# Where the on-chip tiles of a decoder block start: attention's operands 64 bytes apart modulo 128, the down projection's not

## The chip, the cores and the metric

One core of one Trainium2 chip runs the whole kernel. The metric is device time in microseconds (us) of one launch. The kernel before took 448.41 us in the median of three runs (447.92 to 448.52).

## The reference: what is computed

One decoder block on 256 tokens of 1024 channels, all in float32. Cut to what matters here:

```python
h = rmsnorm(x, attn_norm)
proj = h @ w_in                       # latents, MoBA q/k/v, gates
q = rmsnorm(q_lat) @ w_uq             # MLA: 8 heads, 128 plain + 64 rotary features
kv = rmsnorm(kv_lat) @ w_ukv
y_a = causal_attention(q_a, k_a, v_a) @ w_o_mla
y_b = moba_attention(rope(qb), rope(kb), vb) @ w_o_moba   # 256 tokens: one block, so causal attention
x = x + (g_a * y_a + g_b * y_b) @ w_out
h = rmsnorm(x, ffn_norm)
u = causal_dwconv(h @ w_up, conv_w, conv_b)               # 2 x 2816 features
x = x + (silu(u[..., :2816]) * u[..., 2816:]) @ w_down
return rmsnorm(x, final_norm)
```

## The kernel before, in words

Every float32 operand of a matmul is split into a high part in the format fp32r and the rest as a second fp32r tile (`split`, L343: ScalarE casts, VectorE subtracts). A product is then three matmuls, high by high, high by low, low by high (`mm3`, L338). All PE work is made of these triples, besides the transposes of the softmax (float32, with the identity matrix as moving operand) and a few small products.

A matmul has a stationary operand (`lhsT`, 128 columns, brought into the array by a weight load, which the profile shows as engine PEld) and a moving operand (`rhs`, 128, 256 or 512 columns, streamed through). The weight load of the next matmul runs while the current one streams.

Weights come from HBM in units of 1 MB (`unit_plan`) into a ring of three `raw` tiles, and are split into rings of three `whi` and three `wlo` tiles (L329). The stages, with who is stationary and who moves:

- Projections of the input, queries, keys, gates, output products of attention and the up projection (`proj_pair`, `first_unit`, `mqk_unit`, `up_unit`): the weights `whi`/`wlo` are stationary, activations move, 256 columns at a time. The activations are `XH`/`XL`, `LT`, `YBH`/`YBL`, `VH`/`VL`.
- Values and the projection `out` (`proj_tokens`, `mv_unit`): activations are stationary, weights move, 512 columns.
- Attention (`attention`, L592): eight calls of two heads each. Scores: queries (`qh`/`ql`, `qph`/`qpl`) are stationary, keys (`kh`/`kl`, `krh`/`krl`) move, 128 or 256 columns; the rotary scores of MLA take both heads at once, 256 or 512 columns. Values: `VH`/`VL` or `XH`/`XL` (which hold MLA's values then) are stationary, the transposed probabilities `ph`/`pl` move, 256 and 128 columns.
- The down projection (`down`, L835): 11 units of 24 matmuls. The gated products of two feature tiles lie in the ring tiles `qh`/`ql` (L874), which attention no longer needs; they are stationary, and `whi`/`wlo` move, 512 columns. Each unit stands between two units of the up projection; the last two stand together at the end.

The order on each engine is made by `Program.emit` (L208 on) from costs and dependencies; addresses have no part in it. L243 is the one line that issues all of it, so the profile gives that line to nearly every instruction, and groups are told apart by their tiles' names.

A tile takes its place in the order in which it is made, from byte 16512 of each partition (129 times 128) on, its size rounded up to 32 bytes. `T` (L311) and `Ring` (L314) make tiles where the program first asks for them. All sizes but few are multiples of 128 bytes, so nearly every tile starts at one of two remainders modulo 128. In the kernel before:

| start modulo 128 | tiles |
|---|---|
| 0 | `raw`, `whi`, `wlo`, `cst` (tables, identity, mask) |
| 64 | `XH`, `XL`, `VH`, `VL`, `LT`, `YBH`, `YBL`, `qh`, `ql`, `kh`, `kl`, `qph`, `qpl`, `krh`, `krl`, `ph`, `pl`, `e`, `gate`, `ones`, `prm` and the rest |
| 32 | `warm`, `mhalf`, `first` |

The slices that matmuls read start at multiples of 512 bytes within a tile, so that an operand has the remainder of its tile. Two operands are called of one kind here where the remainders are equal, and of two kinds where they are 0 and 64.

Of the kernel before, what the change touches and what calls it, by code (L numbers as in the profile page):

```python
# [20 lines left out]
F32 = mybir.dt.float32  # L21
F32R = mybir.dt.float32r
BF16 = mybir.dt.bfloat16
# [4 lines left out]
D = 1024  # L28
S = 256
H = 8  # L30
# [4 lines left out]
KT = D // 128  # L35
FT = DFF // 128
UNIT = 2048
# [3 lines left out]
NPAR = P_CB + 2 * FT  # L41
# [262 lines left out]
def hybrid_block(ctx: ExitStack, tc: tile.TileContext, x, par, con, fnorm, wpack, out):  # L304
    ctx.enter_context(tc.manual_schedule())
    sb = ctx.enter_context(tc.tile_pool(name="sb", bufs=1))
    ps = ctx.enter_context(tc.tile_pool(name="ps", bufs=1, space=bass.MemoryType.PSUM))
    P = Program(tc.nc)
    act, dve, pool, pe, sp = P.act, P.dve, P.pool, P.pe, P.sp

    def T(name, shape, dt=F32):  # L311
        return sb.tile([128] + shape, dt, tag=name, name=name)

    class Ring:  # L314


        def __init__(self, name, n, shape, dt=F32, space=None):
            self.n = 0
            self.tiles = [(space or sb).tile([128] + shape, dt, tag=f"{name}{j}", name=f"{name}{j}")
                          for j in range(n)]  # L320

        def __call__(self):
            self.n += 1
# [40 lines left out]
    def groups(wv, k, c):  # L364
        return [t.rearrange("p (m k c) -> p m k c", k=k, c=c) for t in wv]

    cst = T("cst", [4 * S + 258])
    cos1, sin1, cos2, sin2 = (cst[:, S * i : S * i + S] for i in range(4))
    ident = cst[:, 4 * S : 4 * S + 128]
# [1 line left out]
    sel = cst[:, 4 * S + 256 :]  # L371


    warm = sb.tile([128, 512], BF16, tag="warm", name="warm")
    pool.memset(warm, 0.0)
    mhalf = T("mhalf", [4])
    pool.memset(mhalf, -0.5)
    ones = T("ones", [128])
    pool.memset(ones, 1.0)
    o = av_bank()  # L380
# [2 lines left out]

    prm = T("prm", [NPAR])
    act.dma_start(prm[:, :KT], par[:, :KT])
    first = T("first", [4])
    act.activation(first, mhalf, AF.Exp)
    xh, xl = T("XH", [KT, S], F32R), T("XL", [KT, S], F32R)

# [31 lines left out]
    smalls = T("smalls", [192])  # L421
    used = [0]

    def small(n):
        used[0] += n
        return smalls[:, used[0] - n : used[0]]

    diag = Ring("diag", 2, [128])
# [64 lines left out]
    gate = T("gate", [16, S])  # L493
# [38 lines left out]
    rbc, c1, s1 = (T(t, [S]) for t in ("rbc", "c1", "s1"))  # L532
# [29 lines left out]
    for j, n in enumerate((QL, KVL)):  # L562
        c = slice(2 * j, 2 * j + 2)
        t = small(2)
# [8 lines left out]
    for f in range(5):  # L573
        g = prm[:, P_QN + f : P_QN + f + 1]
        j = int(f >= 3)
# [5 lines left out]
    krh, krl = (T(t, [2, S], F32R) for t in ("krh", "krl"))  # L581
# [70 lines left out]
    for i in range(4):  # L652
        qh, ql, kh, kl = qhs(), qls(), khs(), kls()
# [78 lines left out]
    for i in range(4):  # L732
        p = slice(2 * i, 2 * i + 2)
        o = proj_pair("oa", i, yah, yal)
        ta = tas()
# [182 lines left out]
```

## Time and profile before

| | |
|---|---|
| median of three runs | 448.41 us (447.92 to 448.52) |
| the profiled execution | 448.98 us |
| its span, first to last instruction | 447.2 us, mean granted TensorE clock 0.994 |
| PE busy (matmuls) | 436.6 us, 98% of the span, 3299 |
| PEld busy (weight loads) | 412.6 us |
| VectorE, ScalarE busy | 356.7 us, 273.3 us |
| PE's share of the chain that ended last | 92% |

PE's busy time counts overlapping matmuls as one stretch, and a matmul's duration includes the way through the array; what a matmul costs in a stream is the time from its start to the next one's start. That interval is read from the timeline, which gives start times to 0.01 us: over many matmuls from the first and the last row and their count.

### The profile page before, as it was taken

The numbers are of one execution on the slowest core, as the hardware profiler recorded it, in microseconds if no ns is written. First come the engines' busy times: TensorE is split into PE (matmuls) and PEld (weight loads), VectorE is DVE, ScalarE is ACT, GpSimd is POOL, SyncE is SP. The second block draws the span as 40 slices with busy tenths as digits, with TensorE's granted clock in tenths as the row PEclk, the third lists the DMA queues.
The fourth block names the chain that finished last, engine by engine and source line by source line (L and its number), as shares of the span: only waits on it lengthen the run. The fifth ranks groups of instructions, "written<-read, shape, count | busy, mean of one in ns | idle before, by whom it ended". The sixth has DMA issues, their size and how long they took to land.

```text
span 447.2 us, 8109 instructions
## 1 busy us (share of the span) xinstructions
PE 436.6 (98%) x3299; PEld 412.6 (92%) x3299; DVE 356.7 (80%) x544; ACT 273.3 (61%) x469; POOL 11.6 (3%) x26
## 2 busy tenths in 40 slices
PE   7999999999999999999999999999999999999992
PEld 5988999999999999999998899999999999999981
DVE  4768998898879987993788569998797797797764
ACT  5686547456645776787665658765565565565523
POOL 0012200000000000000000010000000000000002
PEclk9999999999999999999999999999999999999997
DMA  7985745445453443250478355386555555556002
GB/s 282 394 332 191 281 161 205 141 155 188 139 182 119 152 160 125 94 190 3 164 308 333 136 189 188 102 301 215 191 205 193 198 198 190 188 189 234 2 0 94
DMA packets 12852, 81.75 MB, mean 183 GB/s; under 512 B 1552, under 2 KB 1936, under 8 KB 4112
## 3 DMA queue, kind: packets, MB, share of 16 engines
q1 hardware_dynamic: 12672, 81.25, 50.1%
q8 instruction: 25, 0.41, 0.4%
q14 instruction: 11, 0.09, 0.1%
q10 hardware_dynamic: 144, 0.00, 0.0%
HBM read 80.20 MB, written 1.05 MB: 182 GB/s over the span
## 4 chain that ended last, share of the span: by engine, by line
PE 92%; DVE 2%; DMA 1%; POOL 1%; ACT 1%; issue 1%; SPq 0%; POOLq 0%; ACTq 0%
PE mm L243 66%; PE av L243 14%; PE sc L243 12%; DMA raw<-in_wpack 1%; DVE wlo L243 1%; POOL smalls L243 1%; ACT tb L243 0%; DVE VL L243 0%; SPq L243 0%; DVE gate L243 0%; DVE tb L243 0%; ACT whi L243 0%; ACT B L243 0%; POOLq L913 0%; DVE diag L243 0%
## 5 line engine op out<-in xcount | busy, mean ns | idle before, releaser
L243 DVE TENSOR_TENSOR wlo<-raw,whi 128x1024 fp32r<-128x1024 f32 (+3 forms) x153 | 175.7, 1162 | 35.2 <-ACT whi L243 34.5
L243 ACT CAST whi<-raw 128x1024 fp32r<-128x1024 f32 (+3 forms) x152 | 151.2, 1008 | 84.1 <-PE mm L243 67.4
L243 PE MATMUL mm<-XH,whi 128*128 128x256 f32 x656 | 183.2, 279 | 0.2 <-ACT XH L243 0.2
L243 PE MATMUL mm<-XH,wlo 128*128 128x256 f32 x656 | 181.7, 277 | 0.7 <-DVE wlo L243 0.7
L243 PE MATMUL mm<-XL,whi 128*128 128x256 f32 x656 | 181.6, 277 | 0.1
L243 PEld LDWEIGHTS mm<-XH,whi 128*128 128x128 f32 x656 | 123.2, 188 | 1.5 <-ACT XH L243 1.1
L243 PEld LDWEIGHTS mm<-XH,wlo 128*128 128x128 f32 x656 | 123.2, 188 | 1.1 <-DVE wlo L243 1.1
L243 PEld LDWEIGHTS mm<-XL,whi 128*128 128x128 f32 x656 | 123.4, 188 | 0.8 <-DVE XL L243 0.3
L243 DVE SCALAR_TENSOR_TENSOR tb<-ta,prm,tb 128x255 f32<-128x255 f32 x88 | 40.5, 481 | 2.2 <-ACT tb L243 0.7
L243 ACT ACTIVATE tb<-ta,prm 128x256 f32<-128x256 f32 x44 | 24.2, 595 | 3.8 <-DVE ta L243 3.8
L243 ACT ACTIVATE e<-sc,smalls 128x128 f32<-128x128 f32 (+1 forms) x32 | 13.3, 419 | 12.8 <-DVE smalls L243 11.9
L243 ACT CAST qh<-ta 128x256 fp32r<-128x256 f32 (+1 forms) x26 | 11.4, 437 | 12.3 <-DVE ta L243 12.2
L243 DVE TENSOR_TENSOR ta<-ta,tb 128x256 f32<-128x256 f32 (+1 forms) x35 | 16.9, 484 | 2.2 <-ACT ta L243 0.7
L243 DVE TENSOR_TENSOR ta<-mm,rbc 128x512 f32<-128x512 f32 x22 | 15.2, 690 | 4.2 <-PE mm L243 4.2
L243 PE MATMUL mm<-YBH,whi 128*128 128x256 f32 x64 | 18.1, 283 | 0.0
L243 PE MATMUL mm<-YBH,wlo 128*128 128x256 f32 x64 | 17.7, 277 | 0.0
L243 PE MATMUL mm<-VH,whi 128*128 128x256 f32 x64 | 17.7, 277 | 0.0
L243 PE MATMUL mm<-YBL,whi 128*128 128x256 f32 x64 | 17.7, 277 | 0.0
L243 PE MATMUL mm<-VH,wlo 128*128 128x256 f32 x64 | 17.7, 276 | 0.0
L243 PE MATMUL mm<-VL,whi 128*128 128x256 f32 x64 | 17.7, 276 | 0.0
L243 PE MATMUL sc<-whi,ql 128*128 128x512 f32 x44 | 17.3, 394 | 0.0
L243 PE MATMUL av<-whi,ql 128*128 128x512 f32 x44 | 17.3, 394 | 0.0
(168 smaller groups left out, 736.2 us busy)
## 6 DMA issues: line engine op xcount, KB each, us to landing
raw<-in_wpack SPq DMA_DIRECT2D x66, 1024.0 KB, 4.8
raw<-in_wpack SPq DMA_DIRECT2D x7, 512.0 KB, 7.1
raw<-in_wpack SPq DMA_DIRECT2D x4, 832.0 KB, 4.3
B<-in_x SPq DMA_DIRECT2D x1, 1024.0 KB, 8.9
gate<-in_x SPq DMA_DIRECT2D x1, 1024.0 KB, 4.8
cst<-in_con SPq DMA_DIRECT2D x1, 641.0 KB, 10.0
out<-B SPq DMA_DIRECT2D x2, 320.0 KB, 2.2
raw<-in_wpack SPq DMA_DIRECT2D x2, 256.0 KB, 3.2
```

Source lines behind the costliest of these rows:

```text
L243: getattr(getattr(self.nc, e), method)(*args, **kw)
```

## The change

All tiles are made ahead of the program, in one written order (`homes`); `T` and `Ring` only look them up. `mhalf` and `first` become parts of one tile `lead` of 448 bytes, which ends the first group, and from which on every tile starts 64 bytes past a multiple of 128. The engines' instructions, their order and what they wait for stay the same; only addresses differ.

```diff
+    homes = {}
+    for name, n, shape, dt in (
+        ("raw", 3, [UNIT], F32), ("whi", 3, [UNIT], F32R), ("wlo", 3, [UNIT], F32R),
+        ("qh", 2, [2, S], F32R), ("ql", 2, [2, S], F32R),
+        ("qph", 2, [1, S], F32R), ("qpl", 2, [1, S], F32R),
+        ("ph", 2, [384], F32R), ("pl", 2, [384], F32R),
+        ("lead", 0, [112], F32),
+        ("XH", 0, [KT, S], F32R), ("XL", 0, [KT, S], F32R),
+        ("VH", 0, [2, D], F32R), ("VL", 0, [2, D], F32R),
+        ("YBH", 0, [H, S], F32R), ("YBL", 0, [H, S], F32R),
+        ("kh", 2, [2, S], F32R), ("kl", 2, [2, S], F32R),
+        ("krh", 0, [2, S], F32R), ("krl", 0, [2, S], F32R),
...
+        ("smalls", 0, [192], F32), ("prm", 0, [NPAR], F32), ("cst", 0, [4 * S + 258], F32),
+    ):
+        for t in [f"{name}{j}" for j in range(n)] or [name]:
+            homes[t] = sb.tile([128] + shape, dt, tag=t, name=t)
+
     def T(name, shape, dt=F32):
-        return sb.tile([128] + shape, dt, tag=name, name=name)
+        t = homes[name]
+        assert tuple(t.shape) == (128, *shape) and t.dtype == dt, name
+        return t
...
-            self.tiles = [(space or sb).tile([128] + shape, dt, tag=f"{name}{j}", name=f"{name}{j}")
-                          for j in range(n)]
+            self.tiles = [space.tile([128] + shape, dt, tag=f"{name}{j}", name=f"{name}{j}")
+                          if space else T(f"{name}{j}", shape, dt) for j in range(n)]
...
-    mhalf = T("mhalf", [4])
+    lead = T("lead", [112])
+    mhalf, first = lead[:, 0:4], lead[:, 4:8]
...
-    first = T("first", [4])
```

What this does to the operands that meet in a matmul:

| place | stationary, moving: before | after |
|---|---|---|
| projections, 256 columns | weights 0, activations 64 | the same |
| values and `out`, 512 columns | activations 64, weights 0 | the same |
| scores of attention | queries 64, keys 64 | queries 0, keys 64 |
| probabilities by values | values 64, probabilities 64 | values 64, probabilities 0 |
| down projection, 512 columns | products 64, weights 0 | products 0, weights 0 |
| transposes | `e` 64, identity 0 | `e` 64, identity 32 |

`warm` moves from 32 to 64 and `cst` from 0 to 32; all other tiles keep their remainder.

## Rows read from the trace of the kernel before

**Rows 1.** The page: busy time by engine; the chain that ended last, by line.

```profile
PE 436.6 (98%) x3299; PEld 412.6 (92%) x3299; DVE 356.7 (80%) x544; ACT 273.3 (61%) x469; POOL 11.6 (3%) x26
...
PE mm L243 66%; PE av L243 14%; PE sc L243 12%; DMA raw<-in_wpack 1%; DVE wlo L243 1%; POOL smalls L243 1%; ACT tb L243 0%; DVE VL L243 0%; SPq L243 0%; DVE gate L243 0%; DVE tb L243 0%; ACT whi L243 0%; ACT B L243 0%; POOLq L913 0%; DVE diag L243 0%
```

**Rows 2.** Windows: stretch, busy us (instructions) by engine, granted clock, DMA share, GB/s.

```profile
70.00:142.00 72.00, 72.00 (x634) 72.00 (x633) 61.53 (x91) 40.65 (x75) 0.00 (x0) 1.00 0.46 162
142.00:213.00 71.00, 71.00 (x588) 69.47 (x587) 55.74 (x104) 52.17 (x124) 0.00 (x0) 1.00 0.35 123
213.00:257.00 44.00, 44.00 (x294) 40.04 (x293) 33.64 (x40) 27.61 (x42) 0.00 (x0) 1.00 0.63 239
257.00:437.00 180.00, 180.00 (x1326) 169.49 (x1325) 146.53 (x225) 106.37 (x160) 1.36 (x4) 1.00 0.49 173
```

**Rows 3.** Timeline of PE (start us, duration us, what): a projection unit's 48 matmuls.

```profile
59.20 0.28 PE L243 MATMUL mm<-XH,whi 128*128 128x256 f32 x1
...
64.64 0.28 PE L243 MATMUL mm<-XH,whi 128*128 128x256 f32 x1
```

**Rows 4.** Timeline of PE: scores of one MoBA call, 256 columns, then a gate unit.

```profile
70.87 0.28 PE L243 MATMUL sc<-kl,qh 128*128 128x256 f32 x1
...
71.46 0.28 PE L243 MATMUL mm<-XH,whi 128*128 128x256 f32 x1
```

**Rows 5.** Timeline of PE: scores of one MLA call, then an output product's unit.

```profile
173.18 0.28 PE L243 MATMUL sc<-krl,qph 128*128 128x256 f32 x1
...
174.14 0.40 PE L243 MATMUL sc<-krh,qph 128*128 128x512 f32 x1
174.37 0.40 PE L243 MATMUL sc<-krl,qph 128*128 128x512 f32 x1
174.61 0.39 PE L243 MATMUL sc<-krh,qpl 128*128 128x512 f32 x1
174.84 0.28 PE L243 MATMUL mm<-YBH,whi 128*128 128x256 f32 x1
...
175.52 0.28 PE L243 MATMUL mm<-YBH,whi 128*128 128x256 f32 x1
```

**Rows 6.** Timeline of PE: probabilities by values, then scores, both of 128 columns at the end.

```profile
171.82 0.28 PE L243 MATMUL av<-pl,XH 128*128 128x256 f32 x1
171.94 0.28 PE L243 MATMUL av<-ph,XL 128*128 128x256 f32 x1
172.06 0.23 PE L243 MATMUL av<-ph,XH 128*128 128x128 f32 x1
172.12 0.27 PE L243 MATMUL av<-pl,XH 128*128 128x128 f32 x1
...
172.90 0.28 PE L243 MATMUL sc<-kh,ql 128*128 128x128 f32 x1
```

**Rows 7.** Timeline of PE: a unit of the down projection, 24 matmuls, and the next up unit.

```profile
280.35 0.39 PE L243 MATMUL sc<-whi,qh 128*128 128x512 f32 x1
280.58 0.39 PE L243 MATMUL sc<-wlo,qh 128*128 128x512 f32 x1
...
285.62 0.39 PE L243 MATMUL av<-whi,ql 128*128 128x512 f32 x1
285.85 0.28 PE L243 MATMUL mm<-XH,whi 128*128 128x256 f32 x1
...
286.55 0.28 PE L243 MATMUL mm<-XH,whi 128*128 128x256 f32 x1
```

**Rows 8.** Timeline of PE: the first projection and the values' first half.

```profile
11.30 0.28 PE L243 MATMUL mm<-XH,whi 128*128 128x256 f32 x1
...
23.31 0.40 PE L243 MATMUL av<-whi,XH 128*128 128x512 f32 x1
...
24.02 0.40 PE L243 MATMUL av<-whi,XH 128*128 128x512 f32 x1
...
33.82 0.40 PE L243 MATMUL av<-whi,XH 128*128 128x512 f32 x1
```

**Rows 9.** Timeline of PE: transposes of probabilities, then twelve matmuls of a gate unit.

```profile
78.62 0.49 PE L243 MATMUL sc<-cst,e 128*128 128x128 f32 x3
78.87 0.36 PE L243 MATMUL mm<-XH,whi 128*128 128x256 f32 x1
79.07 0.28 PE L243 MATMUL mm<-XL,whi 128*128 128x256 f32 x1
...
80.36 0.28 PE L243 MATMUL av<-ph,VH 128*128 128x256 f32 x1
```

More of the change, by code (lines that the diff above doesn't have):

```diff
@@ L309, in hybrid_block @@
     act, dve, pool, pe, sp = P.act, P.dve, P.pool, P.pe, P.sp
+    homes = {}
[10 more added lines that the diff above has]
+        ("krh", 0, [2, S], F32R), ("krl", 0, [2, S], F32R),
+        ("LT", 0, [2, 5, S], F32R), ("gate", 0, [16, S], F32), ("B8", 0, [2, D], F32),
+        ("ta", 2, [2, S], F32), ("tb", 2, [2, S], F32),
+        ("diag", 2, [128], F32), ("ones", 0, [128], F32), ("rbc", 0, [S], F32),
+        ("c1", 0, [S], F32), ("s1", 0, [S], F32), ("e", 0, [768], F32),
+        ("warm", 0, [512], BF16),
+        ("smalls", 0, [192], F32), ("prm", 0, [NPAR], F32), ("cst", 0, [4 * S + 258], F32),
+    ):
+        for t in [f"{name}{j}" for j in range(n)] or [name]:
+            homes[t] = sb.tile([128] + shape, dt, tag=t, name=t)
     def T(name, shape, dt=F32):
-        return sb.tile([128] + shape, dt, tag=name, name=name)
+        t = homes[name]
+        assert tuple(t.shape) == (128, *shape) and t.dtype == dt, name
+        return t
     class Ring:
@@ L371, in hybrid_block @@
     sel = cst[:, 4 * S + 256 :]
-    warm = sb.tile([128, 512], BF16, tag="warm", name="warm")
+    warm = T("warm", [512], BF16)
     pool.memset(warm, 0.0)
-    mhalf = T("mhalf", [4])
+    lead = T("lead", [112])
+    mhalf, first = lead[:, 0:4], lead[:, 4:8]
     pool.memset(mhalf, -0.5)
```

## The prediction

> **What bounds the kernel now.** Start with the page: PE is busy 98% of the span, and its matmuls hold 92% of the chain that ended last, 66, 14 and 12 by output [rows 1]. The windows say where that is without a gap: from 70 us to 437 us PE is busy in every microsecond, at a granted clock of 1.00, while VectorE has 14 to 24% of each stretch free and the DMA engines never reach a share of 0.65 [rows 2]. So in these 367 us a nanosecond more or less on a matmul is a nanosecond of the kernel, and nothing else is. The change leaves every instruction, its order and its waits as they were. The one thing it can alter is how long an instruction takes when its operands lie elsewhere, and the view for that is the timeline: the interval between starts in a stream.
>
> Two kinds, 256 columns: a projection unit's 48 matmuls start between 59.20 and 64.64 us, 113.3 ns each [rows 3]. One kind, 256 columns: MLA's scores take 0.96 us for 8 matmuls, 120 ns each [rows 5]; MoBA's take 0.59 us for 5, 118 ns [rows 4]; probabilities by values 0.12 us each [rows 6]. Two kinds, 512 columns: a unit of the down projection is 24 matmuls from 280.35 to 285.85 us, 229 ns each [rows 7]. One kind, 512 columns: only MLA's rotary scores have it. There the first two intervals are 0.23 and 0.24 us, 0.47 for two, 235 ns each, and the third, whose next weights are `whi` and so of the other kind, takes 0.23 [rows 5]. The kind that counts, then, is by my reading that of the moving tile against the weights loaded during it, those of the next matmul.
>
> Two-kind streams have two paces, and the short one is that of the first numbers above. The first projection runs 102 matmuls between 11.30 and 23.31 us at 117.7 ns, with the same tiles as the 113.3 of [rows 3], and hands it on: the values' 42 matmuls from 24.02 to 33.82 us take 233.3 ns and not 229 [rows 8]. It comes back after some transposes: 11 matmuls in 1.29 us, 117 ns, from 79.07 to 80.36 us [rows 9].
>
> **The change part by part.** *Attention.* Eight calls have 108 matmuls of 256 columns (48 plain scores, 12 rotary, 48 with values); in 103 of them the next weights are of one kind now and of two afterwards. At best each goes from 120 to 113.3 ns, 0.69 us; at worst they stream at the long pace, 120 to 117.7, 0.24 us. Half the scores start from 118, so I take 6 ns, 0.6 us. The 85 pairs of 128 columns take 111 ns now (0.78 us for 7 from 172.12 to 172.90 [rows 6]); three transposes and the start behind them, whose operands are not of one kind, take 0.25 us in all [rows 9], which gives no interval, so I bound the gain by 0 and 2 ns (the 113.3 of 256 columns is already above 111) and take 0.1 us. Eight rotary matmuls of 512 columns: 6 ns, 0.05 us. Sum: 0.75 us gained, 0.3 to 0.95. None of it can hide, since PE has no idle time there; nor does it meet a new wait, since the scores lie ahead of whole units of other matmuls, which cover the softmax by more than 5 us (a gate unit of 48 is 5.4 us [rows 3]).
>
> *Down projection.* 11 units of 24 matmuls. The last of a unit meets `whi` weights of an up unit, of one kind already, except between the last two units; that leaves 254 intervals that go from two kinds to one. The nearest row is the rotary one: 235 against 229 ns, 6 ns, 1.5 us lost. The upper bound goes by the full step at 256 columns, 120 against 113.3, 6.7 ns or 1.7 us. Below nothing: a 512-column stream is known at two paces, 233.3 and 229 ns, 4.3 apart [rows 7, 8], and nothing excludes a third as far below: 254 x 4.3 ns, 1.1 us gained. I take the loss because it has the same width, the same remainders and the same next weights; only three matmuls in a row show it.
>
> *The up units behind it.* Ten up pairs follow a down unit. Their first six intervals take 0.70 us [rows 7], against 0.68 after the one-kind rotary scores [rows 5]: 0.2 us gained over ten, if they start as they do there.
>
> *The rest.* Identity, mask and rope tables move to 32 past; 64 transposes read the identity. No row has such an operand in steady state. If each lost what a one-kind pair loses, it is 64 x 6 ns = 0.4 us, if each gained it, 0.4 the other way; I take nothing, because the transposes' three starts fit in 0.25 us [rows 9], less than three of any other stream, and the readers of the tables on VectorE lie beside PE [rows 2]. `warm`, `lead`: seven matmuls ahead of the first weights, covered by the first load.
>
> Sum: -0.75 + 1.5 - 0.2 = +0.55 us. The profiled execution took 448.98 us, 0.57 above the median of the three runs; by the sum it would take 449.5, and the median goes from 448.41 to **449.0 us**, 0.12% more. A measurement of this kernel tells about 0.2%, 0.9 us, from no change. I forecast no measurable change, on the slow side.
>
> **The rivals.** *The one-kind down stream finds a short pace.* Two-kind streams have two paces and need some matmuls to settle [rows 8, 9], and the rotary scores are three matmuls long, so a stream of 24 might settle at 229 ns or lower. Then only the gains are left: -0.75 - 0.2, 447.5 us; with a pace 4.3 ns lower, 446.4. Against it: the second rotary interval is the longer one, 0.24 us [rows 5], and MLA's scores hold 0.12 for eight in a row without coming down.
>
> *Slower: the long pace is handed to the up projection.* After each down unit the up pair streams 96 matmuls without a pause. At 233.3 ns the 512-column stream of [rows 8] carried the long pace across from one shape to the other, and one-kind intervals of 235 ns are near that. If the up streams then stay at 117.7 instead of 113.3 ns, each pair loses 96 x 4.4 ns = 0.42 us, ten lose 4.2, and with the loss of the down units it is 449.0 + 0.2 + 4.2 = 453.4 us. From three pairs on it shows as slower. Against it: the unit after the rotary scores starts at 0.68 us for six, the short pace, at once [rows 5].
>
> *Remainders decide nothing.* Attention's streams are short, change shape from 128 to 256 columns and begin with a start of 0.17 us or so; that alone could put them at a long pace near the 117.7 of [rows 8], as transposes do [rows 9]. Then nothing changes, 448.4 us. Against it: 120 ns is not 117.7, and one unit's matmuls are back at 113.3 right behind the scores [rows 5]. The Trainium skill, "SBUF — State Buffer", section "Who interferes with whom", has this rule: TensorE's two read ports, for the moving operand and for the weight load, are independent, and only VectorE and GpSimd contend. By that rule the change is worth nothing. The difference between [rows 3] and [rows 5] speaks against it, but no row here shows one stream under both placements.
>
> **How the numbers follow.** Forecast 42%: 448.4 to 450.2 us by the bounds above; about 16 of the 42 lie over 449.3, the rest within 0.2%. Short pace in the down stream 28%: 446.4 to 447.7, 24 of them below 447.5. Remainders decide nothing 17%, all within 0.2%. Long pace in the up units 13%, 450 to 453.4. So faster 24%, within 0.2% 47%, slower 29%. The range of 8 in 10 goes from 446.5 to 451.0: it leaves out most of the long-pace case and the far ends of the others. The likeliest case's own range is 448.4 to 450.2.
>
> **What would show it.** In the timeline of the changed kernel: MLA's scores at 113 to 118 ns, not 120, the values' likewise; a down unit from its first to the next up matmul in 5.64 us and not 5.50; the first six up intervals behind it in 0.68; the first projection still at 117.7 or at 113.3 (102 x 4.4 + 48 x 4.3 ns, 0.65 us; which of the two it is I cannot tell from the change). The forecast is wrong if a down unit takes 5.50 us or less, if up pairs take 11.3 us (96 x 117.7 ns) in place of 10.9, or if attention's intervals stay at 120.

## The result, and the profile after

The changed kernel took **452.34 us** (median of four runs, 452.10 to 452.88), the kernel before 448.31 us (447.92 to 448.52) beside it: a ratio of 1.0093, 95% interval 1.0075 to 1.0110. It is slower by 4.0 us, outside the forecast range of 446.5 to 451.0.

The page of the changed kernel answers to [rows 1]: PE is busy longer by 3.6 us, and its share of the chain is 96% where it was 92%.

```profile
PE 440.2 (98%) x3299; PEld 417.1 (93%) x3299; DVE 357.2 (79%) x544; ACT 273.3 (61%) x469; POOL 10.9 (2%) x26
...
PE mm L243 70%; PE av L243 14%; PE sc L243 12%; DMA raw<-in_wpack 1%; POOL smalls L243 1%; ACT tb L243 0%; DVE wlo L243 0%; SPq L243 0%; ACT whi L243 0%; DVE gate L243 0%; ACT B L243 0%; POOLq L940 0%; ACT XH L243 0%; POOLq L243 0%; ACTq L243 0%
```

The last stage's window (stretch, busy us and instructions of PE, PEld, DVE, ACT, POOL, granted clock, DMA share, GB/s) says as before [rows 2] that PE has no idle time and that its granted clock is 1.00. It does 1311 matmuls in the 180 us in which it did 1326.

```profile
257.00:437.00 180.00, 180.00 (x1311) 170.56 (x1309) 145.58 (x223) 105.38 (x157) 1.17 (x3) 1.00 0.49 173
```

The timeline of PE (start us, duration us, what), a down unit and the two up units behind it, answers to [rows 7]. From 297.36 to 302.80 us are 24 matmuls: 226.7 ns each, against 229. From 302.80 to 314.11 us are 96: 117.8 ns each. Before, such a pair (the second block) runs from 302.25 to 313.15 us, 113.5 ns each.

```profile
297.36 0.39 PE L243 MATMUL sc<-whi,qh 128*128 128x512 f32 x1
...
302.80 0.28 PE L243 MATMUL mm<-XH,whi 128*128 128x256 f32 x1
...
314.11 0.39 PE L243 MATMUL sc<-whi,qh 128*128 128x512 f32 x1
```

```profile
302.25 0.28 PE L243 MATMUL mm<-XH,whi 128*128 128x256 f32 x1
...
313.15 0.39 PE L243 MATMUL sc<-whi,qh 128*128 128x512 f32 x1
```

MLA's scores and the unit behind them answer to [rows 5]. Eight intervals from 172.46 to 173.40 us take 0.94 us, against 0.96. The three rotary ones take 0.23, 0.24 and 0.23 us, as before. But the unit behind them streams at the long pace now: from 174.10 to 174.80 us, six in 0.70 us, and from 174.10 to 175.51 us, twelve in 1.41 us, 117.5 ns each.

```profile
172.46 0.29 PE L243 MATMUL sc<-krl,qph 128*128 128x256 f32 x1
...
173.40 0.39 PE L243 MATMUL sc<-krh,qph 128*128 128x512 f32 x1
173.63 0.40 PE L243 MATMUL sc<-krl,qph 128*128 128x512 f32 x1
173.87 0.39 PE L243 MATMUL sc<-krh,qpl 128*128 128x512 f32 x1
174.10 0.28 PE L243 MATMUL mm<-YBH,whi 128*128 128x256 f32 x1
...
174.80 0.28 PE L243 MATMUL mm<-YBH,whi 128*128 128x256 f32 x1
...
175.51 0.40 PE L243 MATMUL mm<-LT,whi 128*128 128x256 f32 x2
```

PE's 3299 matmuls stand in the same order in both traces, so their intervals can be subtracted one by one and summed by stage:

| stage | difference, us |
|---|---|
| start to the first score | -0.62 |
| attention: scores and probabilities by values | -0.34 |
| projections between attention's calls | +0.63 |
| last values of attention to the first down unit | +0.54 |
| down units (228.9 to 226.8 ns each) | -0.55 |
| 864 up matmuls behind down units (113.6 to 117.8 ns each) | +3.61 |
| sum | +3.27 |

The first line is not put down to the change: kernels below that are the same up to the first score differ there by as much as 1.5 us from one execution to the next. Part of it is the pace itself. With the same placement the first projection runs at 117.8 ns in some of the traces below and at 113.3 in others, and the values behind it then at 233.3 or 228.9; the changed kernel's trace is the only one in which they follow 117.8 at 229.0. Without the first line the sum is 3.9 us, within 0.1 us of the 4.0 that was measured.

### The profile page after: what moved, and what is told of

The parts are those of the page before. It is cut to its first block, busy times and chain, and to the rows that moved or that the text cites. A ratio compares the mean times of both kernels' runs of the same rounds, so it can differ in the third digit from the quotient of the medians.

```text
span 450.4 us, 8109 instructions
## 1 busy us (share of the span) xinstructions
PE 440.2 (98%) x3299; PEld 417.1 (93%) x3299; DVE 357.2 (79%) x544; ACT 273.3 (61%) x469; POOL 10.9 (2%) x26
## 4 chain that ended last, share of the span: by engine, by line
PE 96%; DMA 1%; ACT 1%; POOL 1%; DVE 0%; issue 0%; SPq 0%; POOLq 0%; ACTq 0%
PE mm L243 70%; PE av L243 14%; PE sc L243 12%; DMA raw<-in_wpack 1%; POOL smalls L243 1%; ACT tb L243 0%; DVE wlo L243 0%; SPq L243 0%; ACT whi L243 0%; DVE gate L243 0%; ACT B L243 0%; POOLq L940 0%; ACT XH L243 0%; POOLq L243 0%; ACTq L243 0%
## 5 line engine op out<-in xcount | busy, mean ns | idle before, releaser
L243 PEld LDWEIGHTS mm<-XH,wlo 128*128 128x128 f32 x656 | 124.5, 190 | 1.2 <-DVE wlo L243 1.1
L243 ACT CAST qh<-ta 128x256 fp32r<-128x256 f32 (+1 forms) x26 | 11.3, 435 | 11.6 <-DVE ta L243 11.5
L243 PE MATMUL sc<-wlo,qh 128*128 128x512 f32 x44 | 17.1, 389 | 0.0
```

What stands on the lines that cost most here:

```text
L243: getattr(getattr(self.nc, e), method)(*args, **kw)
```

## The experiments

From the part on the place modulo 256 on, starts are given as "64 of 256", the remainder first. A seam is the place where one stream follows another. In the kernel before, the weights and products lie at 128 and 64 of 256, the activations at 64.

**Attention alone, down projection alone.** Which half of the change costs the time? The first takes the products back into a ring of the old kind, in the changed kernel; the second is the kernel before with the products in `LT`'s space, 64 bytes further.

```diff
 # e1, against the changed kernel
-        prods.append((qhs(), qls()))
+        prods.append((khs(), kls()))
 # e2, against the kernel before
+    slots = lt.rearrange("p a b s -> p (a b s)")[:, 16 : 16 + 2048].rearrange(
+        "p (n k s) -> p n k s", k=2, s=S)
-        prods.append((qhs(), qls()))
+        prods.append(tuple(slots[:, 2 * (g % 2) + j] for j in range(2)))
```

> The changed kernel with the products of the down projection in the keys' ring (64) in place of the queries' (0): attention keeps two kinds, the down projection gets two kinds back. Theory A (a one-kind down unit hands the long pace to the up pair behind it): down units back to 5.50 us, up matmuls back to 113.4 ns, the stage from the first down unit on about 3.3 us shorter, 449.0 us. Theory B (the long pace came up at the small products near 266 us and the down units merely carry it): the up pairs stay at 117.7 ns and the down units go to 233 ns, 453 to 454 us.

> The kernel before with one edit: the products lie in the space of LT, which is free by then, 64 bytes further on, so that the down projection has operands of one kind and all else lies as before. Theory A: down units of 227 ns (-0.55 us), up pairs at 117.7 ns from the second unit on (+3.6 to 4.2 us), 451.5 us. Theory B: the stretch before the first down unit ends at the short pace as in the kernel before, so the up pairs stay at 113.4 ns and only the 0.55 us is gained, 447.8 us.

Measured: attention alone 449.25 us, ratio 1.0016 (1.0007 to 1.0026); down alone 451.11 us, 1.0059 (1.0043 to 1.0076). In the timelines, with attention's half alone a down unit (296.62 to 302.12 us) is back at 5.50 us and the up pair behind it at 10.90:

```profile
296.62 0.39 PE L243 MATMUL sc<-whi,kh 128*128 128x512 f32 x1
...
302.12 0.28 PE L243 MATMUL mm<-XH,whi 128*128 128x256 f32 x1
...
313.02 0.39 PE L243 MATMUL sc<-whi,kh 128*128 128x512 f32 x1
```

With the down projection's half alone the down unit takes 5.44 us and the pair 11.31:

```profile
296.99 0.39 PE L243 MATMUL sc<-whi,LT 128*128 128x512 f32 x1
...
302.43 0.28 PE L243 MATMUL mm<-XH,whi 128*128 128x256 f32 x1
...
313.74 0.39 PE L243 MATMUL sc<-whi,LT 128*128 128x512 f32 x1
```

So the products' place alone makes the up units slow, although no matmul of an up unit reads them. In the second kernel attention is as before, and the up units ahead of the first down unit stream at 113.3 ns. The attention half is slightly slower, not faster. The two add up to 1.0075, the lower end of the interval of the whole.

**A kick in the second up unit.** If the up units carry a pace and not a cost of their own, a disturbance should end it. The first matmul of every second up unit is split into two of 128 columns.

```diff
-    def feature_tile(o, m, w, ah, al, ks, first, last):
+    def feature_tile(o, m, w, ah, al, ks, first, last, halves=False):
...
+            if halves and k == ks[0]:
+                r = o[:, S * m : S * m + S]
+                mm(r[:, 0:128], w[0][:, k], ah[:, k, 0:128], first, False)
+                mm(r[:, 128:S], w[0][:, k], ah[:, k, 128:S], False, False)
+                mm(r, w[0][:, k], al[:, k], False, False)
+                mm(r, w[1][:, k], ah[:, k], False, False)
+                continue
...
-                             m == 0 and k == 0, k > 0)
+                             m == 0 and k == 0, k > 0, i % 2 == 1 and m == 0 and k == 0)
```

> The changed kernel, but the first matmul of every second up unit of a pair is done in two halves of 128 columns (one more weight load, 0.11 us each, 11 times), as a disturbance of the stream. After such halves attention's streams come back at the short pace. Theory A: second up units at 113.4 ns, first ones behind a down unit at 117.7 still, since the down unit sets the pace whatever it was entered with: -2.3 + 1.3 us, 451.3 us. Theory B: after the first disturbance all up units stay at 113.4 ns, 449.0 us.

Measured: 451.28 us, ratio 1.0064 (1.0049 to 1.0079). In the timeline the first up unit, from 302.74 us, takes 5.65 us for 48 matmuls; the second has one matmul more and takes 5.56, since all but its first few come at 113.4 ns.

```profile
302.74 0.28 PE L243 MATMUL mm<-XH,whi 128*128 128x256 f32 x1
...
308.39 0.33 PE L243 MATMUL mm<-XH,whi 128*128 128x128 f32 x2
...
313.95 0.39 PE L243 MATMUL sc<-whi,qh 128*128 128x512 f32 x1
```

The same tiles at the same places thus stream at either pace, and one irregular matmul is enough to switch. The down unit behind enters at the short pace, and still the next first up unit is at 117.7 ns: the seam behind a one-kind down unit makes the long pace each time anew.

**One kind everywhere; one half of the products.** What do steady one-kind streams cost? The first kernel is the changed one with `XH` and `XL` moved ahead of `lead`, the products back in their ring. The second is the kernel before with the high products at the weights' remainder and the low ones 64 bytes on from it, so that a down unit's kinds alternate.

```diff
 # e6, in homes
         ("ph", 2, [384], F32R), ("pl", 2, [384], F32R),
+        ("XH", 0, [KT, S], F32R), ("XL", 0, [KT, S], F32R),
         ("lead", 0, [112], F32),
-        ("XH", 0, [KT, S], F32R), ("XL", 0, [KT, S], F32R),
 # e7, against the kernel before
+    flat = lt.rearrange("p a b s -> p (a b s)")
+    slots = [flat[:, a : a + 1024].rearrange("p (n k s) -> p n k s", k=2, s=S) for a in (16, 1056)]
-        prods.append((qhs(), qls()))
+        prods.append(tuple(t[:, g % 2] for t in slots))
```

> The changed kernel with XH and XL at 0 too, so that the 1968 matmuls of 256 columns of the projections from the input and of the up projection are of one kind (and MLA's values with the probabilities as well). If one kind costs in a long stream what it cost in attention's short ones (120 ns against 113.3 or 117.7): 5 to 13 us more, 457 to 465 us. If kinds matter only where streams change: within 1 us of the changed kernel or faster by up to 4.

> The kernel before with the high parts of the products at 0 and the low parts at 64 (both in the space of LT). A down unit then has one-kind and two-kind intervals in turn, and its last stationary operand, a low part, is at 64, while the up weights that follow are at 0. Theory C (the long pace comes where the stationary operand's remainder does not change at the seam, as in the changed kernel, 0 to 0): up pairs start at the short pace, 113.4 ns, and the kernel is within 0.6 us of the kernel before. Theory D (any stream with one-kind intervals hands the long pace on): up pairs at 117.7 ns, 451 to 452 us.

Measured: 462.14 us (one run; 448.59 before) and 450.24 us (one run; 448.50 before). In the first, an up unit takes 5.76 us, 120.0 ns a matmul:

```profile
298.83 0.28 PE L243 MATMUL mm<-XH,whi 128*128 128x256 f32 x1
...
304.59 0.40 PE L243 MATMUL sc<-whi,qh 128*128 128x512 f32 x1
```

The values' one-kind streams of 512 columns take 226.7 ns there. So of the two places one kind is the worse for 256 columns and the better for 512. In the second kernel a down unit takes 5.55 us (297.69 to 303.24), 231 ns a matmul, and the up pair behind it 10.89 (303.24 to 314.13): this mixture hands on the short pace. Its low products lie at 192 of 256, a start that no other kernel so far had, so it isn't a plain mixture of the two kinds. Its span is 1.3 us longer than that of the kernel before (448.5 against 447.2); 0.9 us of it lie ahead of the first score.

**All two kinds, and the place modulo 256.** The aim was the gain alone: queries and probabilities at the weights' remainder, products and rotary queries not. The tables `cst` moved into the first group, so that `lead` has 8 floats.

```diff
 # e8, in homes
-        ("qph", 2, [1, S], F32R), ("qpl", 2, [1, S], F32R),
         ("ph", 2, [384], F32R), ("pl", 2, [384], F32R),
-        ("lead", 0, [112], F32),
+        ("cst", 0, [4 * S + 258], F32), ("lead", 0, [8], F32),
+        ("qph", 2, [1, S], F32R), ("qpl", 2, [1, S], F32R),
 # e8 and all that follow
-        prods.append((qhs(), qls()))
+        prods.append((khs(), kls()))
```

> Only attention's part, without its seams: queries and probabilities at 0, but the rotary queries at 64 like the rotary keys, products in the keys' ring (64), the tables at 0 as before. By theory C the rotary scores, whose stationary operand then changes from 64 to 0 at the seam, hand on the short pace as in the kernel before: attention gains 0.3 us and loses nothing, 448.3 us against 448.6 of the kernel before. If what hands on the long pace is attention's two kinds in general, its projections stay at 117.7 ns after the rotary scores and it is 0.3 us over the kernel before.

Measured: 458.73 us, ratio 1.0228 (1.0211 to 1.0245), which neither theory had. An up unit takes 5.65 us, 117.7 ns:

```profile
296.82 0.28 PE L243 MATMUL mm<-XH,whi 128*128 128x256 f32 x1
...
302.47 0.39 PE L243 MATMUL sc<-whi,kh 128*128 128x512 f32 x1
```

Most projections of the kernel stream like this, but not all: a gate unit of the same trace has 47 intervals in 5.33 us, 113.4 ns, with the same starts modulo 256.

```profile
98.02 0.28 PE L243 MATMUL mm<-XH,whi 128*128 128x256 f32 x1
...
103.35 0.28 PE L243 MATMUL mm<-XH,wlo 128*128 128x256 f32 x1
```

Modulo 128 nothing had been done to these operands. But the second group now started at 192 of 256, not at 64. So `lead` was made 128 bytes longer (40 floats), and for comparison the second group was put at 0 (96 floats), and at 32 and 96 of 256 with `cst` back at the end (104 and 120 floats).

> The run with the rotary queries at 64, which took 458.7 us, had its second group of tiles at 192 past a multiple of 256; the kernels before and after have it at 64, with the weights at 128 in all. Here 128 bytes are added in between, so that the group is at 64 of 256 again; nothing else differs. Theory E (the remainder modulo 256 counts, not modulo 128): projections back to 113.3 ns, the rotary scores hand on the short pace, attention 0.3 us shorter, 448.3 us against 448.6 of the kernel before. If the 458.7 had another cause (the tables at 0, the rotary queries): still over 455 us.

> The changed kernel with products in the second group and that group at 0 past a multiple of 256, 128 bytes from the weights and queries. No row shows this distance: all one-kind pairs so far were at equal remainders modulo 256. If modulo 128 decides, every stream is of one kind: 120 ns and 227 ns, 460 us or more. By theory E it has a pace of its own; between 113 and 120 ns for 256 columns it is 446 to 462 us, and only below 113 ns would it beat the kernel before.

> The changed kernel with the second group of tiles at 32 past a multiple of 128 and products in it. If only equal or unequal remainders matter, projections run at 113.3 or 117.7 ns as at 64, within 1.5 us of the kernel before. If the distance of 64 is what is good, 32 lies between one kind (120 ns) and two, 3 to 13 us slower.

> The same with the second group at 96. If only equal or unequal matters: as at 64, within 1.5 us of the kernel before. If the distance matters and its sign too, it differs from the run at 32; if the sign does not matter, the two agree.

Measured: 448.07 us at 64, ratio 0.9989 (0.9979 to 0.9999); one run each of the others, 462.47 at 0, 460.63 at 32, 461.84 at 96. The time at 0 is what was expected if modulo 128 decides, but the paces are not: 118.7 and 232 ns, where one kind has 120.0 and 226.7. At 64 an up unit is back at 5.44 us (113.3 ns):

```profile
307.99 0.28 PE L243 MATMUL mm<-XH,whi 128*128 128x256 f32 x1
...
313.43 0.39 PE L243 MATMUL sc<-whi,kh 128*128 128x512 f32 x1
```

128 bytes of padding, with every remainder modulo 128 kept, are worth 10.7 us. How much of that is the place of the 256-column streams themselves, and how much a long pace handed to them by the 512-column streams, whose long ones all run at 233 to 234 ns there, is not separated. The kernel at 64 is the gain without the loss: attention's own streams are 0.3 us shorter than before, and all four rotary seams hand on 113.3 ns. Last, its `XH` and `XL` were moved by 16 bytes, to 80 of 256:

```diff
 # e13, against e8b (and 64 floats more for each of the two in homes)
-    xh, xl = T("XH", [KT, S], F32R), T("XL", [KT, S], F32R)
+    xh, xl = (T(t, [KT * S + 64], F32R)[:, 4 : 4 + KT * S].rearrange("p (k s) -> p k s", s=S)
+              for t in ("XH", "XL"))
```

> The kernel of e8b_rotary_64_of_256 with XH and XL 16 bytes further, so that the moving starts lie at 80 of 256 and the weights at 128 (distance 208 instead of 192). Theory J (a distance of exactly 192 is what gives 113.3 ns; its neighbours at 160 and 224 gave 117 to 119): the 256-column streams at 117 to 119 ns, (117.5 - 113.4) x about 2500 such matmuls = +10 us: 455 to 462 us. Rival K (the 16 bytes lie within the same 32- or 64-byte piece and don't count): 113.3 ns and 448 us. Rival L (an optimum lies between 192 and 224): below 113 ns and below 447 us.

Measured: 458.01 us (one run); an up unit takes 5.72 us (295.94 to 301.66), 119.2 ns. Of the distances tried, 113.3 ns holds over most of a kernel only at 192, and in a few units at 64. In the table, "apart" is the moving start less the one of the weights that are loaded meanwhile. `whi` and `wlo` lie at 128 in every kernel, so for most rows the distance and the start itself are not told apart; at distance 0 a pair at 64 (attention before) and one at 128 both come at 120 ns.

| apart, modulo 256 | 256 columns, ns | 512 columns, ns |
|---|---|---|
| 0 | 120.0 | 226.7 |
| 64 | 117.8, in a few units 113.3 | 229 or 233.3 |
| 128 | 118.7 | 232 |
| 160 and 224 | 117 to 120 | no long stream |
| 192 | 113.3 or 117.7 | 233.3 |
| 208 | 119.2 | no stream |

**The end of a down unit.** What at the seam makes the pace? The kernel at 64 of 256 was given products in `LT`'s space, laid out so that only the last 6 of a down unit's 24 matmuls keep the old remainder.

```diff
+    def product_tile(j):
+        return [flat[:, a : a + 2 * w].rearrange("p (t c) -> p t c", c=w)[:, :, :128]
+                for a, w in ((576 * j + 16, 128), (576 * j + 272, 176))]
...
```

> The kernel of e8b_rotary_64_of_256 (448.07 us), but with the products' halves in LT's space, laid out so that 18 of the 24 matmuls of a down unit have their weights' remainder (128 of 256) in the products too, and the last 6 (second feature tile, second half of the tokens) have 64. Theory C (the long pace is handed on where the stationary remainder stays the same from the one-kind stream to the next one): the last 6 matmuls of a down unit hide the seam, so the up pairs behind stay at about 113.4 ns as in the kernel before, while 18 of 24 down matmuls come at 226.7 ns; per down unit 18 x (229.3 - 226.7) = 47 ns less, a few ns of it given back in settling, over 9 units -0.4 to 0 us against e8b: 447.7 to 448.1 us. Rival H (what hands the long pace on is the one-kind stream itself, whatever ends the unit): the up matmuls come at 117.7 as after the change, +3.6 us: about 451.5 us. Rival I: the change of remainder inside a unit costs a new settling each time, down units 231 ns or more as with the low products at 64: 448.2 to 448.9 us.

Measured: 451.45 us, ratio 1.0068 (1.0054 to 1.0081): the long pace again, 11.30 us for the pair. In the timeline the last interval of the unit is 0.23 us long, as the one ahead of it, which says nothing; in whole nanoseconds the trace has 230, 231, 227 at the end. In the kernel before the same threes end on the long one: 226, 229, 231. There the up unit starts with three intervals of 117 and one of 123 ns, and has 113 from the sixth on; here it stays at 118.

```profile
296.41 0.39 PE L243 MATMUL sc<-whi,LT 128*128 128x512 f32 x1
...
301.64 0.39 PE L243 MATMUL av<-whi,LT 128*128 128x512 f32 x1
301.87 0.28 PE L243 MATMUL mm<-XH,whi 128*128 128x256 f32 x1
...
313.17 0.39 PE L243 MATMUL sc<-whi,LT 128*128 128x512 f32 x1
```

That gave a theory: the last interval ahead of the seam decides. It was tried with tails of 2 and 4 (no multiples of three; the last six matmuls in another order, the low or the high products of the second half at 64) and of 12.

```diff
 # e14, against e9; e15 has the two matmuls with l first, and the other half padded
...
+            for n, a, b in ((0, h, w0), (0, h, w1), (1, h, w0), (1, h, w1), (0, l, w0), (1, l, w0)):
+                mm(acc[1, n], a, b[:, 512 * n : 512 * n + 512], False, False)
...
-                for a, w in ((576 * j + 16, 128), (576 * j + 272, 176))]
+                for a, w in ((576 * j + 16, 128), (576 * j + 272, 176 if j % 2 else 128))]
 # e16, against e9
-                for a, w in ((576 * j + 16, 128), (576 * j + 272, 176))]
+                for a, w in ((576 * j + 16, 128), (576 * j + 320, 128))]
```

> As e9_seam_on_new_remainder, but only the last 2 of a down unit's 24 matmuls have their stationary at 64 of 256 (22 at 128, the weights' own); the six matmuls of the last product pair are reordered for that. Theory M (the last interval ahead of the seam decides: 231 ns puts the up unit on the short pace, 227 leaves it on the long one): the last two intervals are 229 and 231, the up units drop to 113.4 ns, and with the down units at 22 x 226.7 + 229 + 231 = 5447 ns instead of 24 x 229 = 5496, 9 units gain 0.4 us against e8b_rotary_64_of_256 (448.07): 447.6 us, ratio 0.998. Rival H (a one-kind stream hands the long pace on whatever ends the unit): up at 117.7 ns, 451.3 us, ratio 1.0065.

> As e14, with the last 4 matmuls at 64 of 256 and 20 at 128. Theory M: intervals 229, 231, 226, 230 at the end, the last one off 226.7 again, so the up units come at 113.4 ns: 447.7 us. If only the 231 counts: 117.7 ns, 451.4 us. Rival H: 451.4 us.

> As e9, with the last 12 matmuls (the whole second feature tile) at 64 of 256 and 12 at 128, in e9's order. Theory M: a multiple of three again, the last interval is 226 to 227, the up units stay at 117.7 ns: 451.6 us. Theory N (the length of the two-kind tail counts; 24 suffice, 6 don't): 113.4 ns is possible, 447.9 us. Rival H: 451.6 us.

Measured: a tail of 2 gives 447.99 us, ratio 0.9996 (0.9985 to 1.0007), a tail of 4 gives 448.04, 1.0000 (0.9989 to 1.0011), a tail of 12 gives 450.98 (one run). With the tail of 2 the down unit takes 5.47 us and the pair 10.90:

```profile
296.03 0.39 PE L243 MATMUL sc<-whi,LT 128*128 128x512 f32 x1
...
301.50 0.28 PE L243 MATMUL mm<-XH,whi 128*128 128x256 f32 x1
...
312.40 0.39 PE L243 MATMUL sc<-whi,LT 128*128 128x512 f32 x1
```

The last intervals are 229, 231 with the tail of 2; 226, 236 with 4; 231, 227 with 12, and the up matmuls come at 113.6, 113.5 and 117.8 ns. All three came out as that theory expected, and the tail's length does not sort them: 2 and 4 bring the short pace, 6 and 12 do not. But the tails of 2 and 4 came together with another order of the last six matmuls, and that order was not run alone, so it remains a rival of the last interval. The down units' gain without the handed-on pace is worth 0.34 us over the whole trace (a unit has 19 of its 24 intervals at 226 to 227 ns, its first three at 231 to 233 and its last two at 229 and 231), too little to show in the time. The one kernel whose interval lies below 1 is the one at 64 of 256 with two-kind products; it beats the kernel before by 0.1%, which is hardly more than nothing.

## Why the prediction was wrong

**The bound was right.** PE without idle time, and a nanosecond of a matmul as a nanosecond of the kernel: the stages' sum without the start, 3.9 us, is the 4.0 that the time shows.

**The step that failed: "The up units behind it".** It put -0.2 us, "if they start as they do there", after the rotary scores. They do not: +3.61 us. The row that it rested on [rows 5] shows three one-kind matmuls whose unit goes on at 113 ns; behind 24 of them all nine pairs stream at 117.8. This is the rival "the long pace is handed to the up projection", which I had at 13% and 4.2 us. Its place and its pace were right, and the experiments on either half and with the kick show them. Its reason was not: it had the long pace carried by down intervals of 235 ns, near the 233.3 of a slow stream, and the units that hand it on run at 226.7, faster than before. Its price counts ten pairs; 864 matmuls are nine, 9 x 0.42 = 3.8 us. What I held against it, the unit behind the rotary scores, went over to its side in the changed kernel itself.

**That the time moved to the forecast's side was luck.** The forecast leaned to slower because of 1.5 us lost in the down units, and these gained.

**The down projection's own step had the wrong sign.** 235 ns from three matmuls, 1.5 us lost; in a steady stream it is 226.7 ns, 0.55 us gained. Only the first unit has longer intervals, 224 to 236 and 231.7 on average in its first nine. So the rival "the one-kind down stream finds a short pace" came true too. I priced these two as exclusive, one with the loss of the down units in it; together they are what happened. Its bound of 4.3 ns below 229 held.

**Attention: the right sign, half the size.** 0.75 us forecast, 0.34 gained. (The upper bound of 0.95 is a slip: its terms make 0.91.) MLA's eight scores went from 0.96 to 0.94 us and not to 0.91: in the call shown they start at 124 ns and are down at 113 to 114 only in the last three. And a term was missing: what follows. The projections between the calls, behind the four rotary seams above all, and the stretch behind attention lost 0.63 and 0.54 us to the long pace. In that stretch no one-kind stream lies ahead, and what sets its pace no run shows. That the attention half alone is 0.16% slower, not faster, says the same. The transposes of the softmax, which the prediction took at nothing, differ by 0.00 us.

**"Remainders decide nothing" fell.** Moving one group of tiles by 128 bytes, with the same instructions, is 10.7 us. The Trainium skill, "SBUF — State Buffer", section "Who interferes with whom", calls TensorE's two read ports independent; these runs contradict the conclusion drawn from it, that placement is worth nothing. Whether it is the ports or something else that the placement changes, no run here shows.

**What was expected of the profile** did tell it: up pairs of 11.3 us and down units under 5.50 were named as signs of a wrong forecast, and both stand in the timeline above. The first projection stayed at 117.8 ns, which the prediction left open.

**Left open.** What inside TensorE makes two paces, and whether the last interval of a down unit chooses one or only goes with it. Where rotary scores are the seam, 231 ns ends them both in the changed kernel (226, 236, 231, long pace behind) and in the one at 64 of 256 (233, 236, 231, short pace behind), so the last interval is not the whole rule. Nor is it where the group lies at 192 of 256: there the down units end on 233 or 234 ns, and the up units behind come at 117.8.

## What to carry to other kernels

In a kernel bound by TensorE, measure the interval of each stream, not only of the one whose operands move: a stream's pace is set partly by the one ahead of it, and a small gain there can cost several times as much behind it. A rival should be priced together with the others that can be true at once. Before padding tiles, note all remainders modulo 256 and change one at a time; here 16 bytes cost 10 us.

## What the runs showed of the hardware that I had not expected

- The remainder modulo 128 is not enough: moving activations at 64 of 256 against weights at 128 stream at 113.3 ns in most of the kernel, at 192 mostly at 117.7, at 80 at 119.2.
- For 512 columns the order turns round: equal remainders modulo 256 are the best of those tried (226.7 ns, against 229 and more), for 256 columns the worst (120.0).
- At one placement a stream of 256 columns can keep either of two paces, 113.3 or 117.7 ns, for 96 matmuls in a row. One matmul split in two ended the long one.
